# Prompt attention of a hybrid decoder layer: both heads of a pair in lock-step, in plain float32 on smaller tiles of the array

## The chip, the core and the metric

The kernel is one launch on one core of a Trainium2 chip. Its time is device time in microseconds (us), from the start to the end of an execution. TensorE (PE in the rows, its weight loads PEld) multiplies, VectorE (DVE), ScalarE (ACT) and GpSimd (POOL) work on elements, and SyncE (SP) issues DMAs. Matmul results land in PSUM, which this kernel cuts into eight banks of 128 partitions by 512 float32: two each of the tags `mm`, `S` and `T`, one each of `A` and `X`.

## The reference

One decoder layer over a prompt of 1024 tokens and 64 sample tokens (8 sequences of 8), width 1024: an input projection, 4 gated linear attention (GLA) heads, 8 softmax heads of width 64 with dilated windows, an output projection, a feed-forward network and norms, all in float32. The change concerns the softmax heads of the prompt:

```python
DILATED_PATTERNS = ((128, 1), (512, 4), (2048, 16))
def dilated_prompt(q, k, v):
    for (W, d) in DILATED_PATTERNS:
        ...
        s = jnp.einsum('brnqhe,brnkhe->brnhqk', qb, kk, preferred_element_type=F32)
        ...
        p = jnp.exp(s - m[..., None])
        den = jnp.sum(p, axis=-1)
        o = jnp.einsum('brnhqk,brnkhe->brnqhe', p.astype(vv.dtype), vv, preferred_element_type=F32)
        parts.append((back(m), back(den), o))
    return combine_patterns(parts)
```

The three patterns of a query are joined by their softmax denominators, so a single softmax over all keys gives the same, with a key that two patterns share counted twice; the kernel has these counts and the ALiBi slopes in a bias table.

## The kernel before, in words

The projection, the GLA heads, the output projection and the feed-forward network run as float32r matmuls of operands that are split in two parts, high and low (`mm3`, lines 203 to 205: high x high, low x high, high x low). The program is recorded through a scheduler that orders each engine's instructions ahead of time; each engine then runs its list in order and waits where an operand is late.

Softmax attention of the prompt goes over 4 pairs of heads (`attn_pair`), in a pair head by head (`for i in range(2)`), in a head over 4 groups `gq` of 256 queries, two tiles `qi` of 128 queries each. For a tile the *near* keys are the 256 keys of its own and the previous tile; the *far* keys are those up to 512 back that stand a multiple of 4 away, gathered by residue modulo 4 in `kres`, 32 per earlier tile and residue. A step of the loop does this:

- Scores into a bank `S`: near ones by two float32r matmuls on the whole array (L858, L859: the rows of the array hold the 64 high and 64 low parts of Q), far ones by four plain float32 matmuls, one for each residue, each into 32 columns of the array (L862).
- Softmax: DVE adds the bias and takes the maximum (L864), ACT the exponential and, with DVE's reciprocal, the scaling (L867 to L869).
- Transposes of the probabilities on TensorE into banks `T` (L881 near, L892 far); ACT copies them out as the high part and DVE subtracts for the low part (L883 and L884 near, L895 and L896 far).
- Values into bank `A`: float32r matmuls on the whole array with V's high and low halves side by side (L904 near, L910 far, once for the high and once for the low part of the probabilities). ACT and DVE add the two halves (L915, L918), and a DMA stores them to `o_dram`.

At a pair's start Q, K and V are split (ACT, DVE and POOL, L785 to L817), and the far values are read back from the output in memory (`vraw`, L839) and split (L841, L842).

Between these stand two other streams. `filler` yields the remaining units of the input projection and of the first half of the output projection, six `mm3` matmuls a unit; `fill_behind` lets so many units go behind a given matmul, at low priority. `sample_steps` does the softmax heads of the sample tokens (L951 key transposes, L959 scores, L995 values, with keys and values from cache by DMA into `raw`), two steps of it after each `gq` of a head.

Of the kernel before, what the change touches and what calls it, by code (L numbers as in the profile page):

```python
# [11 lines left out]
F32 = mybir.dt.float32  # L12
F32R = mybir.dt.float32r
# [24 lines left out]
FILL_START = (169, 202, 237, 277)  # L38
FILL_FROM = (164, 204, 240, 281)
FILL_TO = (199, 242, 273, 306)  # L40
# [4 lines left out]
FILL_STAGE = (1.0, 2.0, 3.0)  # L45
FILL_END = (26, 25, 19, 24)
# [59 lines left out]
def hymba_layer(  # L106
# [653 lines left out]
    PT = [[att.tile([P, 4, P], F32R, name=f"PT{part}{j}") for part in ("hi", "lo")] for j in range(2)]  # L760

    klo = [att.tile([P, T], F32R, name=f"klo{i}") for i in range(2)]
    Vf = att.tile([P, 2, 4, P], F32R, name="Vf")
    PF = {m: [att.tile([P, 2, P], F32R, name=f"PF{part}{m}") for part in ("hi", "lo")] for m in (P, 64)}
    for a in (klo[0][64:], klo[1][:64], Vf[64:, 1], PF[64][0][64:], PF[64][1][64:]):
        pool.memset(a.bitcast(F32), 0.0)

    def fill_upto(p, stage):
        part = (3 * (stage // 3) + FILL_STAGE[stage % 3]) / FILL_END[p]
        return FILL_FROM[p] + (FILL_TO[p] - FILL_FROM[p]) * min(1, part)  # L770

    def attn_pair(p):
        fs = slice(p * P, (p + 1) * P)
        fill(156 + 36 * p)
        fill_behind(latest[0], FILL_START[p])
        qr, kr, vr = (raws[p][name] for name in "qkv")
        Q, K, V = [], [], []
# [4 lines left out]
        for i in range(2):  # L782
            own, oth = slice(64 * i, 64 * i + 64), slice(64 - 64 * i, 128 - 64 * i)
            k = att.tile([P, T], F32R, tag="K", name="K", bufs=2)
# [3 lines left out]
            q = att.tile([P, T], F32R, tag="Q", name="Q", bufs=2)  # L788
            qv = q.rearrange("p (w r u) -> p w r u", r=4, u=32)
            src = qr[own, :T].rearrange("p (w u r) -> p w r u", r=4, u=32)  # L790
            for r in range(4):
                act(out=qv[own, :, r, :], in_=src[:, :, r, :], func=AF.Copy)
                vec.tensor_tensor(out=qv[oth, :, r, :], in0=src[:, :, r, :], in1=qv[own, :, r, :].bitcast(F32), op=ALU.subtract)
            K.append(k)
            Q.append(q)
            V.append(att.tile([P, NTT, P], F32R, tag="V", name="V", bufs=2))
# [3 lines left out]
        pool.tensor_copy(out=knew, in_=kr[:, T:])  # L800


        for t0 in range(0, NTT, 4):
            for src, dst in ((kr, ckp), (vr, cvp)):
# [3 lines left out]
                stg = smp.tile([P, 4, P], F32, tag="raw", name="stg", bufs=6)  # L808
                pv = ps.rearrange("p (t f) -> p t f", f=P)
                act(out=stg, in_=pv, func=AF.Copy)  # L810
                dma(out=dst[:, t0 : t0 + 4, fs], in_=stg)
                if src is vr:
                    for i in range(2):
                        hs = slice(64 * i, 64 * i + 64)
                        vhi = V[i][:, t0 : t0 + 4, 0:64]
                        act(out=vhi, in_=stg[:, :, hs], func=AF.Copy)
                        vec.tensor_tensor(out=V[i][:, t0 : t0 + 4, 64:128], in0=stg[:, :, hs], in1=vhi.bitcast(F32), op=ALU.subtract)  # L817
# [7 lines left out]
        dma(out=cvs[:, fs], in_=vnew)  # L825


        rows = cv_prompt[0, 0].rearrange("(c r) h e -> c r h e", r=4)

        fill_behind(last, FILL_FROM[p])  # L830

        sample = sample_steps(p, qbd, knew, vnew)
        for i in range(2):
            own, oth = slice(64 * i, 64 * i + 64), slice(64 - 64 * i, 128 - 64 * i)
            bias = att.tile([P, 480], F32, tag="bias", name="bias", bufs=1)
            dma(out=bias, in_=bias_p[2 * p + i])
            vraw = smp.tile([P, 2, 4, 64], F32, tag="raw", name="vraw", bufs=6)
            for cb, n in ((0, P), (1, 64)):
                dma(out=vraw[:n, cb], in_=rows[cb * P : cb * P + n, :, 2 * p + i])  # L839
                vh = Vf[:n, cb, :, 0:64]  # L840
                pool.tensor_copy(out=vh, in_=vraw[:n, cb])  # L841
                vec.tensor_tensor(out=Vf[:n, cb, :, 64:], in0=vraw[:n, cb], in1=vh.bitcast(F32), op=ALU.subtract)  # L842

            kres = att.tile([P, 4, 224], F32, tag="kres", name="kres", bufs=1)
            src = kr[own, : 4 * 224].rearrange("p (c r) -> p r c", r=4)
            pool.tensor_copy(out=kres[own], in_=src)
            pool.tensor_copy(out=kres[oth], in_=src)
            for gq in range(NTT // 2):
                Ps = []
                for qi in (2 * gq, 2 * gq + 1):  # L850
                    qs = slice(qi * P, (qi + 1) * P)
                    nf = 32 * qi if qi > 1 else 0
                    n = nf + (256 if qi else P)
                    k0 = max(qi - 1, 0) * P
                    sb = att.tile([P, 480], F32, tag="P", name="P", bufs=3)
                    st = att.tile([P, 3], F32, tag="st", name="st", bufs=4)
                    ps = bank("S")
                    mm(out=ps[:, nf : nf + 256], lhsT=Q[i][:, qs], rhs=K[i][:, k0 : k0 + 256], start=True, stop=False)  # L858
                    last_s = mm(out=ps[:, nf : nf + 256], lhsT=Q[i][:, qs], rhs=klo[i][:, k0 : k0 + 256], start=False, stop=True)  # L859
                    for r in range(4 if nf else 0):  # L860
                        q0 = qi * P + 32 * r
                        last_s = mm(out=ps[32 * r : 32 * r + 32, :nf], lhsT=Q[i][:, q0 : q0 + 32].bitcast(F32),  # L862
                                    rhs=kres[:, r, :nf], start=True, stop=True)
                    vec.tensor_tensor_reduce(  # L864
                        out=sb[:, :n], in0=ps[:, :n], in1=bias[:, 480 - n :] if qi else bias[:, 352:480], scale=-1.0,
# [359 lines left out]
```

## Time and profile before

| | |
|---|---|
| median of 3 runs | 1622.61 us (1622.34 to 1630.09) |
| profiled execution, its own time | 1624.35 us |
| its span, first to last instruction | 1622.6 us |
| PE busy | 1547.1 us, 95% of the span |
| PEld, DVE, ACT, POOL busy | 1429.8, 792.2, 491.2, 308.8 us |
| mean granted clock of TensorE | 0.972 of 2.4 GHz |

Busy time of PE counts each matmul until its results have left the array, so back-to-back matmuls overlap in it, and 95% doesn't mean that the array multiplies 95% of the time. What a matmul costs the next one is the distance between two starts. A plain float32 matmul stands in the trace as two records, a float32r matmul or a transpose as one.

### The profile page before, as it was taken

The page shows a single profiled execution, that of the slowest core. Times are in us where ns is not written, and L with a number is a line of the kernel's source. Part 1 is how long each engine was busy: PE and PEld are TensorE (multiplying, and loading weights), DVE is VectorE, ACT ScalarE, POOL GpSimd, SP SyncE. Part 2 cuts the span into 40 slices and gives each one's busy share as a digit, 9 for nine tenths or more (in the row PEclk, how much of TensorE's full clock was granted, in tenths as well). Part 3 has the DMA queues.
Part 4 walks back from the last instruction along what each step waited for, and adds up shares of the span by engine and source line. Part 5 has one row for each costly group of instructions (what it writes and reads, how often), then busy time and mean ns, then how long its engine had stood idle before and what let it go on. Part 6 is the DMA issues. An engine that isn't in the chain of part 4 may idle for free.

```text
span 1622.6 us, 28319 instructions
## 1 busy us (share of the span) xinstructions
PE 1547.1 (95%) x11696; PEld 1429.8 (88%) x11696; DVE 792.2 (49%) x1700; ACT 491.2 (30%) x995; POOL 308.8 (19%) x325
## 2 busy tenths in 40 slices
PE   7979999989899998998999999999999999999997
PEld 6768878888677876777999999999999999999997
DVE  5495575564534536345743444434344443434436
ACT  3143232145445456453522111121202112120213
POOL 1493342052213111100511000000100000010002
PEclk9998999989999998999999999999999999999998
DMA  5320121153353345666421021011102111110102
GB/s 151 97 70 28 30 67 42 42 147 108 91 135 103 87 127 169 181 172 200 122 79 53 26 66 49 30 53 40 53 27 65 41 38 53 37 55 27 53 1 111
DMA packets 180881, 126.71 MB, mean 78 GB/s; under 512 B 21104, under 2 KB 172560, under 8 KB 180752
## 3 DMA queue, kind: packets, MB, share of 16 engines
q1 hardware_dynamic: 176544, 124.69, 25.8%
q8 instruction: 92, 1.51, 0.4%
q10 hardware_dynamic: 4208, 0.21, 0.2%
q14 instruction: 37, 0.30, 0.1%
HBM read 101.40 MB, written 23.46 MB: 77 GB/s over the span
## 4 chain that ended last, share of the span: by engine, by line
PE 82%; DVE 8%; DMA 6%; issue 1%; POOL 1%; ACT 1%; SPq 0%; DVEq 0%; ACTq 0%; POOLq 0%
PE ps_mm L203 12%; PE ps_mm L204 12%; PE ps_mm L205 12%; PE ps_S L203 5%; PE ps_S L205 5%; PE ps_S L204 5%; PE ps_T L204 2%; PE ps_T L203 2%; PE ps_T L205 2%; DMA raw<-in_cache_swa_v_dram 2%; PE ps_A L910 2%; PE ps_A L205 1%; PE ps_A L203 1%; PE ps_A L204 1%; PE ps_X L204 1%
## 5 line engine op out<-in xcount | busy, mean ns | idle before, releaser
L203 PE MATMUL ps_mm<-xhi,whi 128*128 128x384 f32 (+1 forms) x576 | 202.3, 353 | 3.8 <-DVE raw_v L238 1.8
L1087 POOL TENSOR_TENSOR gt<-gt,ut 128x384 f32<-128x384 f32 (+1 forms) x66 | 64.0, 970 | 700.6 <-DVE ut L1086 700.6
L204 PE MATMUL ps_mm<-xlo,whi 128*128 128x384 f32 (+1 forms) x576 | 196.3, 342 | 0.2 <-DVE xlo L280 0.2
L205 PE MATMUL ps_mm<-xhi,wlo 128*128 128x384 f32 (+1 forms) x576 | 195.4, 341 | 0.6 <-DVE wlo L175 0.6
L203 PE MATMUL ps_mm<-hhi,whi 128*128 128x384 f32 (+1 forms) x528 | 173.5, 329 | 1.2 <-DVE gt L1084 1.2
L205 PE MATMUL ps_mm<-hhi,wlo 128*128 128x384 f32 (+1 forms) x528 | 173.7, 329 | 0.0
L204 PE MATMUL ps_mm<-hlo,whi 128*128 128x384 f32 (+1 forms) x528 | 173.6, 329 | 0.0
L203 PE MATMUL ps_S<-hhi,whi 128*128 128x384 f32 (+1 forms) x528 | 172.7, 327 | 0.0
L204 PE MATMUL ps_S<-hlo,whi 128*128 128x384 f32 (+1 forms) x528 | 172.7, 327 | 0.0
L205 PE MATMUL ps_S<-hhi,wlo 128*128 128x384 f32 (+1 forms) x528 | 172.5, 327 | 0.0
L203 PEld LDWEIGHTS ps_mm<-xhi,whi 128*128 128x128 f32 x576 | 112.2, 195 | 13.1 <-issue 5.6
L1085 ACT ACTIVATE gt<-gt 128x384 f32<-128x384 f32 (+1 forms) x66 | 33.1, 502 | 296.3 <-DVE gt L1084 296.3
L205 PEld LDWEIGHTS ps_mm<-xhi,wlo 128*128 128x128 f32 x576 | 112.0, 195 | 4.8 <-issue 2.6
L204 PEld LDWEIGHTS ps_mm<-xlo,whi 128*128 128x128 f32 x576 | 112.6, 196 | 3.8 <-issue 2.5
L1086 DVE TENSOR_TENSOR ut<-ps_S,rstd_bc 128x384 f32<-128x384 f32 (+1 forms) x66 | 35.4, 536 | 162.0 <-PE ps_S L205 162.0
L203 PEld LDWEIGHTS ps_mm<-hhi,whi 128*128 128x128 f32 x528 | 99.8, 189 | 1.4 <-DVE gt L1084 1.4
L205 PEld LDWEIGHTS ps_mm<-hhi,wlo 128*128 128x128 f32 x528 | 99.9, 189 | 0.0
L204 PEld LDWEIGHTS ps_mm<-hlo,whi 128*128 128x128 f32 x528 | 99.7, 189 | 0.0
L204 PEld LDWEIGHTS ps_S<-hlo,whi 128*128 128x128 f32 x528 | 99.2, 188 | 0.0
L203 PEld LDWEIGHTS ps_S<-hhi,whi 128*128 128x128 f32 x528 | 99.2, 188 | 0.0
L205 PEld LDWEIGHTS ps_S<-hhi,wlo 128*128 128x128 f32 x528 | 99.2, 188 | 0.0
L174 ACT ACTIVATE ghi<-gt 128x384 fp32r<-128x384 f32 (+1 forms) x66 | 33.5, 507 | 214.0 <-POOL gt L1087 214.0
(353 smaller groups left out, 3425.1 us busy)
## 6 DMA issues: line engine op xcount, KB each, us to landing
wraw<-in_w_in_dram SPq DMA_DIRECT2D x22, 512.0 KB, 3.8
wraw<-in_w_ffn_gate_dram SPq DMA_DIRECT2D x22, 512.0 KB, 3.6
wd_raw<-in_w_ffn_down_dram SPq DMA_DIRECT2D x22, 512.0 KB, 3.2
wuraw<-in_w_ffn_up_dram SPq DMA_DIRECT2D x22, 512.0 KB, 3.6
raw<-in_cache_swa_k_dram SPq DMA_DIRECT2D x32, 256.0 KB, 5.3
raw<-in_cache_swa_v_dram SPq DMA_DIRECT2D x32, 256.0 KB, 4.3
xa<-x_dram SPq DMA_DIRECT2D x32, 192.0 KB, 3.0
xr<-in_x_prompt_dram SPq DMA_DIRECT2D x8, 512.0 KB, 8.4
```

Of the source, the lines that this page charges most:

```text
L174: a = by.tensor_copy(out=hi, in_=raw) if by else act(out=hi, in_=raw, func=AF.Copy)
L203: mm(out=ps, lhsT=whi[k], rhs=xhi[k], start=first and k == 0, stop=False)
L204: mm(out=ps, lhsT=whi[k], rhs=xlo[k], start=False, stop=False)
L205: mm(out=ps, lhsT=wlo[k], rhs=xhi[k], start=False, stop=last and k == n - 1)
L910: mm(out=o, lhsT=Vf[:, cb, r, :], rhs=part[:, :, 32 * r : 32 * r + 32], start=False, stop=False)
L1085: act(out=gt, in_=gt, func=AF.Silu)
L1086: vec.tensor_tensor(out=ut, in0=pu[:, :n], in1=rstd_bc[:, cs], op=ALU.mult)
L1087: pool.tensor_tensor(out=gt, in0=gt, in1=ut, op=ALU.mult)
```

## The change

Both heads of a pair go through a step together. Q and K are no longer split: POOL reorders Q into `qres` (all 128 partitions, 64 a head) and K into `kres`, and the scores of the two heads are plain float32 matmuls on tiles of 64 rows by 32 columns, eight to a step: two heads (the array's rows) by four residues (its columns), into two banks `S`. The probabilities are copied out of the transposes once, and values are plain float32 matmuls on tiles of 128 rows by 64 columns, head 0 in the left half of the array and head 1 in the right half, both into one bank `A`. V is read where the transposes left it, and the far values are loaded for both heads at once. Softmax, transposes and the arithmetic on scores stay, as do the filler's 312 units; the marks at which they are let go are spread evenly, and the sample's steps come four to a `gq`.

```diff
+        qres = att.tile([P, T], F32, tag="qres", name="qres", bufs=2)
+        kres = att.tile([P, 4, 224], F32, tag="kres", name="kres", bufs=2)
+        for w in range(0, NTT, 4):
+            ws = slice(w * P, (w + 4) * P)
+            pool.tensor_copy(out=qres[:, ws].rearrange("p (w r u) -> p w r u", r=4, u=32),
+                             in_=qr[:, ws].rearrange("p (w u r) -> p w r u", r=4, u=32))
+        pool.tensor_copy(out=kres, in_=kr[:, : 4 * 224].rearrange("p (c r) -> p r c", r=4))
...
-            act(out=k[own], in_=kr[own, :T], func=AF.Copy)
-            pool.tensor_copy(out=k[oth], in_=kr[own, :T])
-            vec.tensor_tensor(out=klo[i][own], in0=kr[own, :T], in1=k[own].bitcast(F32), op=ALU.subtract)
...
-                act(out=qv[own, :, r, :], in_=src[:, :, r, :], func=AF.Copy)
-                vec.tensor_tensor(out=qv[oth, :, r, :], in0=src[:, :, r, :], in1=qv[own, :, r, :].bitcast(F32), op=ALU.subtract)
...
+        for cb, n in ((0, P), (1, 64)):
+            dma(out=vf[:n, cb], in_=rows[cb * P : cb * P + n, :, fs])
...
+        def scores(qi):
...
+            ps = [bank("S") for _ in heads]
+            for part in range(2 if nf else 1):
+                for r in range(4):
+                    rs = slice(32 * r, 32 * r + 32)
+                    for i, own in enumerate(heads):
+                        out = ps[i][rs, :nf] if part else ps[i][rs, nf:n]
+                        rhs = kres[own, r, :nf] if part else kr[own, k0 : k0 + near]
+                        ins = mm(out=out, lhsT=qres[own, qi * P + 32 * r : qi * P + 32 * r + 32], rhs=rhs, start=True, stop=True)
...
-                    mm(out=ps[:, nf : nf + 256], lhsT=Q[i][:, qs], rhs=K[i][:, k0 : k0 + 256], start=True, stop=False)
-                    last_s = mm(out=ps[:, nf : nf + 256], lhsT=Q[i][:, qs], rhs=klo[i][:, k0 : k0 + 256], start=False, stop=True)
...
+                if gq:
+                    act(out=av, in_=pv, func=AF.Copy)
...
+                    vec.tensor_copy(out=PF[m][i][:m], in_=ps[:m, 2 * cb * P : (2 * cb + 2) * P].rearrange("p (x q) -> p x q", x=2))
...
+                for i, own in enumerate(heads):
+                    last = mm(out=av[own, a:b], lhsT=V[:, kt, own], rhs=pt[i][:, e : e + (b - a) // P, :],
+                              start=j == 0, stop=j == len(steps) - 1)
+                for cb, m in far if j == 0 else ():
+                    for r in range(4):
+                        for i, own in enumerate(heads):
+                            o = av[own, :256].rearrange("p (x q) -> p x q", x=2)[:, :, 32 * r : 32 * r + 32]
+                            mm(out=o, lhsT=vf[:, cb, r, own], rhs=PF[m][i][:, :, 32 * r : 32 * r + 32], start=False, stop=False)
...
+                vec.tensor_copy(out=sum_[:, xs].rearrange("p (u r) -> p r u", r=4), in_=av[:, xs].rearrange("p (r u) -> p r u", r=4))
```

TensorE's list in the first pair, before, where scores and values of two steps meet (`PThi`, `PTlo`: near probabilities, `PFhi`, `PFlo`: far ones, `raw`: cached keys of the sample):

```order
L904 MATMUL ps_A<-PTlo_3833,V 128x256
L951 MATMUL ps_T<-ident,raw 128x128 x4
L910 MATMUL ps_A<-PFhi_3839,Vf 128x2x32
L858 MATMUL ps_S<-K,Q 128x256
L859 MATMUL ps_S<-klo_3834,Q 128x256
L862 MATMUL ps_S<-kres,Q 32x224 x3
L910 MATMUL ps_A<-PFlo_3840,Vf 128x2x32
```

and the same engine in the first pair now (L200 to L202 are the filler's lines, L835 scores, L890 far values, L933 the sample's key transposes):

```order
L202 MATMUL ps_mm<-xhi,wlo 128x320
L835 MATMUL ps_S<-raw_k,qres 32x256
L890 MATMUL ps_A<-PF_3834,Vf_3830 64x2x32
L933 MATMUL ps_T<-ident,raw 128x128 x4
L835 MATMUL ps_S<-raw_k,qres 32x256 x4
L890 MATMUL ps_A<-PF_3835,Vf_3830 64x2x32
```

Where only L862 stood on narrow tiles, every score and every value matmul does now, in two shapes, 64 by 32 and 128 by 64; one of a step's eight score matmuls stands alone ahead of a value matmul.

VectorE's list at the start of the first pair, before (`Q`, `klo`: low parts; `raw_v` is a filler unit's result on its way out of PSUM):

```order
L787 TENSOR_TENSOR klo_3834<-raw_k,K 64x1024
L175 TENSOR_TENSOR wlo<-wraw,whi 128x1024
L793 TENSOR_TENSOR Q<-raw_q,Q 64x8x32
L238 TENSOR_TENSOR raw_v<-ps_mm,rstd_bc 128x384
L793 TENSOR_TENSOR Q<-raw_q,Q 64x8x32 x3
L787 TENSOR_TENSOR klo_3835<-raw_k,K 64x1024
L793 TENSOR_TENSOR Q<-raw_q,Q 64x8x32 x4
```

and now, with buffer numbers (L840 is the softmax's first pass, L235 the filler's):

```order
L172 TENSOR_TENSOR wlo_3844<-wraw_3840,whi_3843 128x1024
L235 TENSOR_TENSOR raw_v_3847<-ps_mm_3848,rstd_bc_81 128x384
L840 ISA P_3956,st_3957<-ps_S_3946,bias_3942 128x128
L840 ISA st_3957 128x1
L840 ISA P_3962,st_3963<-ps_S_3947,bias_3944 128x128
```

The passes that split Q and K are gone from the list, and the first softmax passes follow the filler's result at once.

TensorE's list at the start of the last pair, now, with buffer numbers (`ps_S_7289` and `ps_S_7290` are the two heads of one step, `ps_S_7336` is head 0 of the next; L794 are the pair's own transposes):

```order
L794 MATMUL ps_T_7019<-ident_71,raw_v_5620 128x128 x4
L835 MATMUL ps_S_7094<-raw_k_5890,qres_7004 32x256 x4
L984 MATMUL ps_T_6938<-ident_71,avs_6936 128x128
L835 MATMUL ps_S_7289<-raw_k_5890,qres_7004 32x256 x4
L835 MATMUL ps_S_7289<-kres_7005,qres_7004 32x64 x4
L794 MATMUL ps_T_7026<-ident_71,raw_k_5890 128x128 x4
L835 MATMUL ps_S_7290<-raw_k_5890,qres_7004 32x256 x4
L835 MATMUL ps_S_7290<-kres_7005,qres_7004 32x64 x4
L794 MATMUL ps_T_7034<-ident_71,raw_v_5620 128x128 x4
L835 MATMUL ps_S_7336<-raw_k_5890,qres_7004 32x256 x4
```

Here the two heads don't stand together: each block of scores has one head, four tiles of the eight, and few other instructions lie between the blocks.

## Rows read from the trace of the kernel before

**Rows 1.** Busy time by stretch: attention, with the filler (start, length, engines, clock, DMA).
```profile
315.00:750.00 435.00, 407.84 (x3299) 333.73 (x3299) 205.89 (x536) 209.64 (x472) 91.23 (x89) 0.95 0.47 132
```
**Rows 2.** TensorE's waits in 315 to 750 us: total, times, longest, us.
```profile
PE ps_T L951 <- DMA raw<-in_cache_swa_k_dram: 4.0, 5, 1.2
PE ps_S L858 <- DVE Q L793: 3.3, 2, 2.7
...
PE ps_A L904 <- DVE PTlo L884: 2.7, 4, 1.2
...
PE ps_mm L203 <- DVE raw_v L238: 1.8, 1, 1.8
```
**Rows 3.** TensorE's groups by shape in 315 to 750 us.
```profile
L910 PE MATMUL ps_A<-PFhi,Vf 128*128 128x64 f32 x128 | 31.0, 270 | 0.0
...
L858 PE MATMUL ps_S<-K,Q 128*128 128x256 f32 x64 | 23.7, 372 | 6.4 <-DVE Q L793 3.3 <-DVE st L864 3.0
...
L904 PE MATMUL ps_A<-PThi,V 128*128 128x128 f32 x56 | 14.9, 287 | 0.0
...
L904 PE MATMUL ps_A<-PThi,V 128*128 128x256 f32 x32 | 11.9, 370 | 1.2 <-ACT PThi L883 1.2
...
L862 PE MATMUL ps_S<-kres,Q 128*32 128x224 f32 x64 | 8.3, 391 | 0.0
```
**Rows 4.** Timeline of TensorE, a run of far values (start us, duration us).
```profile
705.91 0.28 PE L910 MATMUL ps_A<-PFhi,Vf 128*128 128x64 f32 x1
...
706.58 0.42 PE L203 MATMUL ps_mm<-ohi,whi 128*128 128x384 f32 x1
```
**Rows 5.** The same timeline, a stream of plain float32 on four column tiles.
```profile
715.12 1.30 PE L995 MATMUL ps_X<-raw,pT 128*32 128x128 f32 x40
```
**Rows 6.** The same timeline, in and out of narrow tiles.
```profile
707.71 0.28 PE L858 MATMUL ps_S<-K,Q 128*128 128x256 f32 x1
707.83 0.28 PE L859 MATMUL ps_S<-klo,Q 128*128 128x256 f32 x1
708.04 0.37 PE L862 MATMUL ps_S<-kres,Q 128*32 128x96 f32 x8
708.34 0.39 PE L858 MATMUL ps_S<-K,Q 128*128 128x256 f32 x1
708.56 0.28 PE L859 MATMUL ps_S<-klo,Q 128*128 128x256 f32 x1
708.77 0.43 PE L862 MATMUL ps_S<-kres,Q 128*32 128x128 f32 x8
709.13 0.44 PE L982 MATMUL ps_T<-ident,sb 128*128 128x128 f32 x2
```
**Rows 7.** The same timeline in GLA: from one narrow shape to another.
```profile
225.45 0.76 PE L607 MATMUL ps_S<-Z 64*32 64x32 f32 x64
226.13 0.55 PE L677 MATMUL ps_T<-V,ktok 128*64 128x128 f32 x6
```
**Rows 8.** The same timeline in GLA: head 0's eight records on one tile, then head 1's.
```profile
97.59 0.96 PE L633 MATMUL ps_S<-Z 64*64 64x64 f32 x16 [0.41 <-DVE Z L625]
```
**Rows 9.** Timeline of VectorE at the start of attention.
```profile
349.42 3.60 DVE L793 TENSOR_TENSOR Q<-raw_q,Q 64x256 fp32r<-64x256 f32 x4
353.06 0.56 DVE L238 TENSOR_TENSOR raw_v<-ps_mm,rstd_bc 128x384 f32<-128x384 f32 x1
```
**Rows 10.** Timeline of TensorE there.
```profile
353.67 0.44 PE L203 MATMUL ps_mm<-xhi,whi 128*128 128x384 f32 x1 [1.83 <-DVE raw_v L238]
...
357.00 0.58 PE L858 MATMUL ps_S<-K,Q 128*128 128x256 f32 x1 [1.80 <-DVE st L864]
```
**Rows 11.** Busy time by stretch: two in which the granted clock fell.
```profile
356.20:366.40 10.20, 8.68 (x53) 6.60 (x53) 3.94 (x17) 5.23 (x15) 1.38 (x2) 0.50 0.71 180
...
438.10:448.40 10.30, 8.82 (x43) 7.42 (x43) 5.01 (x16) 5.53 (x16) 1.90 (x1) 0.50 0.27 78
```
**Rows 12.** VectorE's groups by shape, attention: a softmax pass.
```profile
L864 DVE CUSTOM_DVE_ANT_0 P<-ps_S,bias 128x256 f32<-128x256 f32 x8 | 3.4, 422 | 3.5 <-PE ps_T L892 3.5
```
**Rows 13.** GpSimd's groups by shape, attention: the reordering of K.
```profile
L846 POOL COPY kres<-raw_k 64x896 f32<-64x896 f32 x8 | 16.3, 2038 | 51.4 <-PE ps_S L862 51.4
```

More of the change, by code (lines that the diff above doesn't have):

```diff
@@ L807, in attn_pair @@
                     nc.tensor.transpose(out=ps[:, j * P : (j + 1) * P], in_=src[:, (t0 + j) * P : (t0 + j + 1) * P], identity=ident)
[L808 to L817, printed above, removed]
+                rows = V[:, t0 : t0 + 4] if src is vr else smp.tile([P, 4, P], F32, tag="raw", name="stg", bufs=6)
+                act(out=rows, in_=ps.rearrange("p (t f) -> p t f", f=P), func=AF.Copy)
+                dma(out=dst[:, t0 : t0 + 4, fs], in_=rows)
         ps = bank("T")
@@ L898, in attn_pair @@
-                fill_behind(last, fill_upto(p, 12 * i + 3 * gq + 1))
-                av = bank("A")
-                steps = [(2 * gq, 0, 256, 1)] + ([(2 * gq - 1, 0, P, 0)] if gq else []) + [(2 * gq + 1, P, 256, 3)]
-                for j, (kt, a, b, e) in enumerate(steps):
-                    for part in (hi, lo):
-                        last = mm(out=av[:, a:b], lhsT=V[i][:, kt, :], rhs=part[:, e : e + (b - a) // P, :],
-                           start=j == 0 and part is hi, stop=j == len(steps) - 1 and part is lo)
-                    for cb, m in far if j == 0 else ():
-                        for r in range(4):
-                            o = av[:, :256].rearrange("p (x q) -> p x q", x=2)[:, :, 32 * r : 32 * r + 32]
-                            for part in PF[m]:
-                                mm(out=o, lhsT=Vf[:, cb, r, :], rhs=part[:, :, 32 * r : 32 * r + 32], start=False, stop=False)
@@ L911, in attn_pair @@
-                fill_behind(last, fill_upto(p, 12 * i + 3 * gq + 2))
-                latest[0] = last
-                half = att.tile([P, 256], F32, tag="half", name="half", bufs=1)
-                sum_ = att.tile([P, 256], F32, tag="sum", name="sum", bufs=2)
-                act(out=half[own], in_=av[oth, :256], func=AF.Copy)
-                for x in range(2):
-                    vw = lambda a: a[own, x * P : x * P + P]
-                    vec.tensor_tensor(out=vw(sum_).rearrange("p (u r) -> p r u", r=4), in0=vw(av).rearrange("p (r u) -> p r u", r=4),
-                                      in1=vw(half).rearrange("p (r u) -> p r u", r=4), op=ALU.add)
@@ L920, in attn_pair @@
-                f0 = 512 + p * P + 64 * i
-                dma(out=o_dram[f0 : f0 + 64, gq * 256 : gq * 256 + 256], in_=sum_[own])
-                next(sample, None)
+                if gq:
+                    act(out=av, in_=pv, func=AF.Copy)
+                else:
+                    act(out=a[:, 1:4], in_=ps[:, P:].rearrange("p (e q) -> p e q", q=P), func=AF.Copy)
+                pt.append(a)
+            far = [(cb, min(P, 64 * gq - cb * P)) for cb in range(-(-64 * gq // P))]
+            for i in range(2 if far else 0):
+                ps = bank("T")
+                for cb, m in far:
+                    for x in range(2):
+                        last = nc.tensor.transpose(out=ps[:m, (2 * cb + x) * P : (2 * cb + x + 1) * P],
+                                                   in_=Ps[x][i][0][:, cb * P : cb * P + m], identity=ident)
+                    vec.tensor_copy(out=PF[m][i][:m], in_=ps[:m, 2 * cb * P : (2 * cb + 2) * P].rearrange("p (x q) -> p x q", x=2))
@@ new lines, in outputs @@
+            tick(last)
+            latest[0] = last
+            sum_ = att.tile([P, 256], F32, tag="sum", name="sum", bufs=2)
+            for x in range(2):
+                xs = slice(x * P, x * P + P)
+                vec.tensor_copy(out=sum_[:, xs].rearrange("p (u r) -> p r u", r=4), in_=av[:, xs].rearrange("p (r u) -> p r u", r=4))
+            dma(out=o_dram[512 + p * P : 512 + (p + 1) * P, gq * 256 : gq * 256 + 256], in_=sum_)
+        sample = sample_steps(p, qbd, knew, vnew)
+        for gq in range(NTT // 2):
+            Ps = [scores(2 * gq), scores(2 * gq + 1)]
+            outputs(gq, Ps)
+            for _ in range(4):
```

132 lines of the change are left out of this document (48 added, 84 removed).

## The prediction

> **What bounds the kernel now.** I read the stretches first. Attention and the filler that runs with it take 435 us, 315 to 750 us, at a mean clock of 0.95 [rows 1]; the change touches nothing outside. TensorE is busy for 408 of them, DVE for 206, ACT for 210, POOL for 91: TensorE's list bounds the stretch. Its waits come next [rows 2]: they are short and many, the cache's DMA 4.0 us for the keys, split operands that are late (`Q` 3.3, `PTlo` 2.7), and a filler result behind DVE's queue 1.8. So the question is what the same work costs on the array, by starts and not by busy time. The group list gives counts and shapes [rows 3], the timeline the prices [rows 4 to 8].
>
> **Prices.** A float32r matmul costs 0.112 us however few its columns: six far-value matmuls of 64 columns take 0.67 us from start to start [rows 4], and one of 256 columns takes 0.12 [rows 6]. Plain float32 on four column tiles goes through in ten steps of four records: 1.30 us less some 0.27 for the last to leave [rows 3, 5] is nine steps, 0.11 us a record of 128 columns. A matmul has two records, so a column costs 1.72 ns on its tile, and tiles of one shape run beside each other. A block of narrow matmuls therefore costs 1.72 ns times the columns of its busiest tile.
>
> Going in and out costs extra [rows 6]. L859 is followed after 0.21 us where 0.12 is usual (+0.09); the eight records of 96 columns should take 2 x 0.082 and the next starts after 0.30 (+0.14); that next one holds the array for 0.22 (+0.10). A round trip to float32r costs 0.33 us. Out to a transpose the middle part is 0.36 against 0.22, so 0.23 or more with the way in; I take 0.28. From one narrow shape to another [rows 7] the next start comes 0.08 us before the last block's end, where 0.16 is usual [rows 6]: 0.08, and I take 0.10. Its bounds are 0.08 and a whole trip, 0.33.
>
> **The change on the array.** I counted blocks along TensorE's lists, for the whole of attention.
>
> - Values. Before: 176 near and 256 far matmuls (the groups shown and their like) at 0.112, 48.4 us. Now: 64 blocks with 16,896 columns on the busiest tile, 29.1 us. That is -19.3. Far values carry it: their price was the 128-column weight load and not their 64 columns.
> - Scores. Before: 128 near matmuls at 0.112, 14.3 us, and 65 blocks of far ones with 9,824 columns, 16.9 us. Now 76 blocks with 19,232 columns, 33.1 us, so +1.9. If no block were broken up it would be 11,136 columns, 19.2 us; the list at the last pair's start shows why it isn't, one head at a time.
> - Trips. Before, 99 to float32r and 57 to transposes: 32.7 + 16.0 = 48.7 us. Now 80 and 96, 26.4 + 26.9, and 73 changes between narrow shapes at 0.10, 7.3: 60.6 us. +11.9, and from 5.8 - 48.7 + 53.3 = +10.4 to +28.7 by the bounds.
>
> Together -5.5 us. Filler, transposes and the sample's matmuls are the same in number and price.
>
> The Trainium skill has a rule that speaks against the change: TensorEngine Tiling (Array Packing), "Key Properties", says that changing the tiling mode drains TensorE, while tiles of one mode run independently. The trace agrees on entering and leaving (0.33 us); on a change between two narrow shapes it shows 0.08 and not a whole drain. By the rule taken at its word each of the 73 would cost 0.33, 16.8 us more; that is the fourth rival.
>
> **Waits.** At the start of attention DVE splits Q for 3.60 us in one run, and the filler's result `raw_v` stands behind it in DVE's queue [rows 9]; TensorE waits 1.83 us for that and 1.80 for the first softmax [rows 10]. DVE's list now has neither split. What takes their place is `qres` on POOL: K's 896 columns take 2.04 us there [rows 13], so 512 of Q take about 1.2, from a projection long done. I count the waits of `Q` and `raw_v`, 5.1 us [rows 2], as gone. Of `PTlo`'s 2.7 half stays, since ACT's copy is still ahead. -6.4.
>
> New are waits for the `S` banks. Both heads of a step now hold the two banks until DVE's first pass has read them, 0.42 us and 0.08 to read out for each head at 256 columns [rows 12], about 1.0 us for both. Behind the waiting matmul stands everything on TensorE, the sample's keys and the filler too. Between 24 of the 31 successive steps the list holds 2.3 us or more of other work, by the prices above; between seven it holds 0.7 or less, four of them in the last pair. Seven times 0.6 is +4; the bounds are 0 and 31 x 1.0.
>
> The far values are now read by TensorE from the loaded tile, with no split. The load stands on SP behind the store of V, and its first use is one `gq` later, so I cost it at nothing; SP's DMAs of the prompt's attention fall from 80 to 56. If that cover were gone, a wait as long as the cache's longest, 1.2 us [rows 2], in each pair: 5 us.
>
> **Clock.** A mean of 0.95 over 435 us means some 43 us at 1.2 GHz, half speed. Two falls of 10 us each come right after the waits at the start of attention and at the first change of pair [rows 11]. Work at half speed costs as much again, up to 22 us in all. The first follows waits that I count as gone; I take one fall, with what the new waits bring in set against it: -4, between -15 and +8.
>
> **Sum.** -5.5 - 6.4 + 4 - 4 = -11.9 us. The profiled execution took 1624.35 us, 1.75 more than its span and 1.74 above the median of the runs. From the median, 1622.6 - 11.9 is 1610.7. I predict 1611 us.
>
> **Rivals.**
>
> 1. The banks `S` decide: the steps run in lock-step with DVE. From 0.78 us at each of 31 gaps, 24 us in place of 4, the time passes 1630; at the full 1.0 us it is 1638. For it: seven gaps that are nearly empty, and blocks that alternate heads. Against it: the long gaps elsewhere, and a DVE that loses the split passes. 9%.
> 2. The array gives what I count, but waits and clock don't move, since the remaining waits (cache DMA) set the falls: -5.5 + 4 or so, 1617 to 1623. For it: the cache's waits are as long as `Q`'s [rows 2]. 22%.
> 3. The two heads don't run beside each other. Then the busiest column counts, 28,544 in place of 19,232, +16.0: 1627. The trace has head 0's and head 1's tiles side by side only at a hand-over [rows 8]: 16 records of 64 columns, 0.055 each, would take 0.88 + 0.22 in succession, and took 0.96. That they overlap at all speaks against it. 8%.
> 4. Changes between narrow shapes cost a whole trip: +16.8, 1628. Rows 7 speak against it. 5%.
> 5. More comes back: shorter chains behind ACT and DVE remove most falls of the clock, -10 to -15 in place of -4: 1600 to 1604, and below. For it: DVE had been the late engine at both falls. 15%.
>
> The forecast itself, 1605 to 1617, has 41%.
>
> **How the numbers follow.** A difference under about 0.5%, 8 us, can't be told from none here, so faster is under 1614.5 and slower over 1630.7. Faster: rival 5 and some 37 of the forecast's 41 points, 0.52. Slower: most of rival 1 and the upper ends of 3 and 4, 0.13. The rest, 0.35, is the same. The range leaves out a tenth at each side: from 1596, where two more falls of the clock are gone, to 1630, which takes in rivals 2 to 4.
>
> **What would show it.** In the profile after: far values at two records of some 0.055 us per 64 columns side by side; the eight score matmuls of a step starting within 0.1 us of each other, both heads, and the next start some 0.45 us after the block's first for 256 columns; attention's stretch 9 to 15 us shorter; no wait of TensorE for `raw_v` at its start and fewer low-clock stretches. It is wrong if the heads' records follow each other in time, if TensorE waits over 10 us in total for L840, or if the narrow blocks' changes cost more than 0.2 us each.

## The result

The changed kernel takes 1587.32 us (median of 4 runs, 1585.57 to 1589.02); the kernel before took 1624.47 beside it (4 runs). The ratio is 0.977, with a 95% interval from 0.975 to 0.980: 37 us faster, three times the forecast of 12, and below the range that was given. The direction was right and the size wrong.

The head of the page of the changed kernel:

```profile
span 1586.4 us, 28631 instructions
...
PE 1522.2 (96%) x12080; PEld 1377.2 (87%) x12080; DVE 717.3 (45%) x1556; ACT 435.6 (27%) x867; POOL 272.1 (17%) x296
```

TensorE is busy 25 us less (1547.1 before) although it has 384 records more. The stretches tell where the rest is. The next rows are those of the kernel before, from the first transpose of attention to its last matmul, and from there to the first matmul of the feed-forward part (start, length, busy time of PE, PEld, DVE, ACT, POOL, then clock, DMA share, GB/s):

```profile
315.10:743.60 428.50, 402.18 (x3259) 328.47 (x3258) 202.93 (x525) 208.15 (x469) 91.23 (x89) 0.95 0.47 132
743.60:812.70 69.10, 63.68 (x384) 61.54 (x384) 44.13 (x81) 34.64 (x69) 22.64 (x21) 1.00 0.51 156
```

and the same two of the changed kernel, which answer to [rows 1]:

```profile
308.50:710.00 401.50, 388.95 (x3691) 285.79 (x3691) 135.37 (x388) 154.11 (x344) 53.24 (x60) 0.98 0.51 142
710.00:778.10 68.10, 58.63 (x337) 57.46 (x336) 41.13 (x74) 33.55 (x65) 22.84 (x21) 0.95 0.49 151
```

Length minus busy time is TensorE's idle time: 31.7 us before, 22.0 now. At the low level the granted clock is 0.50, 1.2 GHz. The falls in these stretches are, before, the two of [rows 11] and

```profile
591.70:595.20 3.50, 3.50 (x21) 3.11 (x20) 0.79 (x3) 2.15 (x6) 0.00 (x0) 0.51 0.50 104
...
629.30:642.90 13.60, 11.58 (x54) 9.22 (x55) 10.07 (x28) 8.41 (x20) 1.36 (x4) 0.50 0.64 212
...
673.70:680.50 6.80, 5.22 (x24) 4.29 (x25) 3.62 (x11) 2.59 (x6) 0.15 (x1) 0.50 0.56 169
```

and now

```profile
631.70:635.10 3.40, 3.40 (x22) 2.74 (x10) 0.56 (x1) 0.53 (x1) 0.00 (x0) 0.50 0.47 126
679.50:689.70 10.20, 10.08 (x60) 5.96 (x60) 0.98 (x3) 0.00 (x0) 0.00 (x0) 0.50 0.28 82
727.20:734.00 6.80, 4.07 (x13) 4.07 (x14) 1.70 (x4) 1.55 (x4) 0.00 (x0) 0.50 0.02 6
```

As the cost of low clock I count half of TensorE's busy time in them (at the low level the 384-column matmuls of a filler unit start 0.32 us apart, otherwise 0.17): 37.8 us busy before and 17.6 now, so 18.9 and 8.8. Idle time in a fall is counted as idle time only. What is left is work: 447.0 and 438.8. Together 497.6 and 469.6, 28.0 us less. I use this split for every kernel below. Another 6.6 us lie ahead of attention, where the two programs are the same, and 1.6 behind it.

TensorE's waits before, 315 to 812.6 us (total, times, longest), where [rows 2] leaves them out:

```profile
PE ps_X L995 <- DMA raw<-in_cache_swa_v_dram: 4.1, 5, 1.4
...
PE ps_mm L203 <- ACT ohi L174: 3.6, 2, 2.3
...
PE ps_S L858 <- DVE st L864: 3.0, 3, 1.8
PE ps_mm L203 <- DVE xa L520: 2.9, 1, 2.9
...
PE ps_T L892 <- DVE osT L1007: 1.8, 2, 1.3
```

and in the changed kernel, 308 to 779 us, which answer to [rows 2]:

```profile
PE ps_mm L200 <- ACT ohi L171: 9.1, 4, 6.7
PE ps_X L977 <- DMA raw<-in_cache_swa_v_dram: 2.9, 2, 1.9
PE ps_T L933 <- DMA raw<-in_cache_swa_k_dram: 2.6, 1, 2.6
PE ps_A L890 <- DVE PF L876: 2.0, 1, 2.0
PE ps_T L863 <- ACT stg L796: 2.0, 1, 2.0
```

No wait of the score matmuls (L835) for their banks is in the whole list; nor is one for `raw_v`, for the softmax pass (`st` L864, 3.0 us before) or for the projection's `xa` (2.9 before). The projection's operand `ohi` is waited for longer, 9.1 us against 3.6: that is given back.

The groups that take the place of [rows 3], and the timeline that shows their price (start, duration):

```profile
L835 PE MATMUL ps_S<-raw_k,qres 64*32 64x256 f32 x448 | 31.4, 388 | 0.0
...
L884 PE MATMUL ps_A<-PT,V 128*64 128x256 f32 x64 | 20.7, 405 | 0.0
...
L890 PE MATMUL ps_A<-PF,Vf 128*64 128x64 f32 x256 | 16.7, 237 | 2.0 <-DVE PF L876 2.0
```
```profile
445.94 0.66 PE L933 MATMUL ps_T<-ident,raw 128*128 128x128 f32 x4
446.53 0.66 PE L835 MATMUL ps_S<-raw_k,qres 64*32 64x256 f32 x16
446.98 0.43 PE L835 MATMUL ps_S<-kres,qres 64*32 64x160 f32 x2
447.35 0.32 PE L941 MATMUL ps_X<-kT,qbd 128*32 128x128 f32 x4
```

Sixteen records of 256 columns are eight matmuls, four of each head. From their start to the next is 0.45 us, as forecast; one matmul alone should take 256 x 1.72 = 0.44, and two on each of four tiles 0.88. So the eight tiles run beside each other, both heads too. One matmul of 160 columns should take 0.28 and the next shape starts after 0.37: a change between narrow shapes costs 0.09. Over the whole attention the medians are 0.09 there, 0.09 into narrow tiles, 0.20 out to float32r and 0.15 out to a transpose.

### The profile page after: what moved, and what is told of

It is laid out like the page before. It is cut to its first block, busy times and chain, and to the rows that moved or that the text cites. A ratio compares the mean times of both kernels' runs of the same rounds, so it can differ in the third digit from the quotient of the medians.

```text
span 1586.4 us, 28631 instructions
## 1 busy us (share of the span) xinstructions
PE 1522.2 (96%) x12080; PEld 1377.2 (87%) x12080; DVE 717.3 (45%) x1556; ACT 435.6 (27%) x867; POOL 272.1 (17%) x296
## 4 chain that ended last, share of the span: by engine, by line
PE 86%; DMA 5%; DVE 5%; POOL 1%; issue 1%; ACT 1%; SPq 0%; DVEq 0%; ACTq 0%; POOLq 0%
PE ps_mm L200 13%; PE ps_mm L201 12%; PE ps_mm L202 12%; PE ps_S L202 5%; PE ps_S L201 5%; PE ps_S L200 5%; PE ps_T L201 2%; PE ps_T L200 2%; PE ps_T L202 2%; PE ps_S L835 2%; DMA oraw<-o_dram 2%; PE ps_T L933 2%; PE ps_X L977 2%; PE ps_A L202 1%; PE ps_A L200 1%; PE ps_A L201 1%
## 5 line engine op out<-in xcount | busy, mean ns | idle before, releaser
L200 PE MATMUL ps_mm<-xhi,whi 128*128 128x384 f32 (+1 forms) x576 | 199.5, 347 | 2.0 <-ACT whi L171 1.6
L202 PE MATMUL ps_mm<-xhi,wlo 128*128 128x384 f32 (+1 forms) x576 | 194.6, 339 | 1.1 <-DVE wlo L172 1.1
L200 PE MATMUL ps_mm<-hhi,whi 128*128 128x384 f32 (+1 forms) x528 | 172.8, 327 | 1.2 <-DVE gt L1066 1.2
L202 PE MATMUL ps_mm<-hhi,wlo 128*128 128x384 f32 (+1 forms) x528 | 173.0, 328 | 0.0
L200 PE MATMUL ps_S<-hhi,whi 128*128 128x384 f32 (+1 forms) x528 | 172.7, 327 | 0.0
L202 PE MATMUL ps_S<-hhi,wlo 128*128 128x384 f32 (+1 forms) x528 | 172.5, 327 | 0.0
L200 PEld LDWEIGHTS ps_mm<-xhi,whi 128*128 128x128 f32 x576 | 110.2, 192 | 13.6 <-issue 7.6
L202 PEld LDWEIGHTS ps_mm<-xhi,wlo 128*128 128x128 f32 x576 | 110.2, 191 | 7.3 <-issue 4.8
L200 PEld LDWEIGHTS ps_mm<-hhi,whi 128*128 128x128 f32 x528 | 99.2, 188 | 1.4 <-DVE gt L1066 1.4
L202 PEld LDWEIGHTS ps_mm<-hhi,wlo 128*128 128x128 f32 x528 | 99.2, 188 | 0.0
L202 PEld LDWEIGHTS ps_S<-hhi,wlo 128*128 128x128 f32 x528 | 99.2, 188 | 0.0
L200 PEld LDWEIGHTS ps_S<-hhi,whi 128*128 128x128 f32 x528 | 99.2, 188 | 0.0
L1090 DVE TENSOR_TENSOR h<-h,ps_T 128x384 f32<-128x384 f32 (+1 forms) x120 | 63.5, 529 | 68.1 <-PE ps_T L202 68.1
```

The costliest lines, as they stand in the source:

```text
L200: mm(out=ps, lhsT=whi[k], rhs=xhi[k], start=first and k == 0, stop=False)
L202: mm(out=ps, lhsT=wlo[k], rhs=xhi[k], start=False, stop=last and k == n - 1)
L1090: vec.tensor_tensor(out=h[:, k, cs], in0=h[:, k, cs], in1=ps[:, :n], op=ALU.add)
```

## The experiments

The prices just given make a count possible for any kernel here: TensorE's instruction list, each block at its busiest tile, each change of shape at its price. "Counted" below means this. The table comes first, since the readings use it. All but the first column are from the profiled execution, over the two stretches shown above, in us.

| kernel | median | start | length | idle | low clock | work |
|---|---|---|---|---|---|---|
| before | 1624 | 315.1 | 497.6 | 31.7 | 18.9 | 447.0 |
| changed | 1587.3 | 308.5 | 469.6 | 22.0 | 8.8 | 438.8 |
| after2 | 1591.8 | 313.6 | 468.0 | 18.2 | 11.6 | 438.3 |
| b_nosplit | 1615.5 | 310.8 | 493.0 | 24.6 | 21.5 | 447.0 |
| b_nolo | 1600.8 | 310.7 | 474.1 | 25.9 | 13.6 | 434.7 |
| b_sum_q2 | 1608.0 | 313.3 | 484.4 | 22.2 | 18.1 | 444.1 |
| b_nolo_q | 1601.8 | 315.0 | 476.4 | 25.5 | 20.2 | 430.6 |
| a_heads | 1613.5 | 313.7 | 484.6 | 17.3 | 7.6 | 459.7 |
| a_pair | 1594.9 | 309.5 | 473.7 | 23.5 | 10.8 | 439.4 |
| a_passes | 1622.4 | 315.0 | 498.8 | 37.2 | 22.5 | 439.1 |
| a_passes_q2 | 1620.8 | 315.1 | 496.0 | 36.6 | 19.5 | 439.9 |
| a_passes_q3 | 1612.7 | 315.3 | 490.3 | 28.1 | 20.6 | 441.6 |
| after_q | 1585.9 | 310.3 | 461.4 | 22.3 | 9.9 | 429.2 |
| a_block2 | 1578.5 | 309.6 | 453.2 | 20.5 | 10.7 | 422.0 |
| a_block3 | 1557.7 | 314.1 | 433.6 | 20.7 | 4.5 | 408.3 |
| a_block3_q2 | 1562.2 | 308.3 | 441.2 | 22.9 | 9.9 | 408.4 |

The two profiles of the changed kernel (changed, after2) differ by 3.8 us in idle time and 2.8 in low clock, so less than that is not read. A profiled execution can lie off its kernel's median: b_nolo's is 5.9 us below it, a_block2's 5.3, a_heads's 4.9, after_q's 3.8, and a_passes_q3's 3.4 above. Beside the runs below the kernel before took 1623.4 to 1626.9 us (medians).

**Is the gain ahead of attention the change's?** after2 is the changed kernel, unedited.

> The changed kernel once more, unchanged. Theory A (the 6.6 us by which attention starts earlier, 308.5 against 315.1 us, are a clock fall that comes or stays away from execution to execution, and not the change): the start of attention moves by some us between the two executions of one kernel, up to 6.8 us, one fall more or less ahead of it. Rival (something in the changed program moves it): the start is again within 1 us of 308.5 us, with the same falls at 103, 116, 144 and 249 us. Total 1585 to 1590 us.

Measured: 1591.76 us in one run, just over the 1590 given, with attention's start at 313.6. Here falls of the clock stand at 211.5 and 252.4 us for 6.8 us each, where the first profile had one of 3.4 at 249.4. So the 6.6 us belong to the execution and not to the change; the stretch that the change touches is 28.0 and 29.6 us shorter in the two profiles.

**Take the passes away.** In the kernel before, b_nolo leaves out every VectorE pass that makes a low part for the prompt's attention (the filler's stay); b_nosplit only those at the pair starts. The low tiles are set to zero once:

```diff
-            vec.tensor_tensor(out=klo[i][own], in0=kr[own, :T], in1=k[own].bitcast(F32), op=ALU.subtract)
-                vec.tensor_tensor(out=qv[oth, :, r, :], in0=src[:, :, r, :], ...)
-                        vec.tensor_tensor(out=V[i][:, t0 : t0 + 4, 64:128], ...)
-                vec.tensor_tensor(out=Vf[:n, cb, :, 64:], ...)
 # b_nolo also:
-                    vec.tensor_tensor(out=lv[:, xs, ys_, :], in0=pv[:, xs, ys_, :], ...)
-                        vec.tensor_tensor(out=flo[:m], in0=pv, ...)
```

> The kernel before, with its float32r operands and its matmuls, all of them, but without VectorE's passes that make low parts: those tiles are set to zero once, so the low parts are left out of the sums. Theory A (the 9.7 us of waits and 10.1 us of low clock that the change saved beyond the array work hang on these passes): idle time of TensorE in the attention stretch falls from 31.7 to 20 to 24 us, the low-clock time from 44 us towards 20 us, and the total to 1605 to 1612 us. Rival B (they hang on the lock-step, half as many steps with twice the cover): no more than 4 us come off, 1620 to 1626 us.

Measured: 1600.81 us, ratio 0.987 (0.985 to 0.990), 22.6 us less than before. More than theory A gave, and it came in another way: in the profile idle falls by 5.8, to 25.9 where 20 to 24 was given, low clock by 5.3, and the work by 12.3 although every matmul is still there. The list shows why. With fewer passes to wait for, the program's scheduler breaks the blocks up less (TensorE goes into narrow tiles 138 times instead of 155, for far scores and the sample's matmuls), and the count gives 12.0 less. Of the waits that don't name a removed pass not all went:

```profile
PE ps_X L991 <- DMA raw<-in_cache_swa_v_dram: 5.0, 7, 1.2
...
PE ps_mm L203 <- DVE xa L520: 3.8, 3, 1.8
PE ps_T L947 <- DMA raw<-in_cache_swa_k_dram: 3.6, 4, 2.2
...
PE ps_S L856 <- DVE st L862: 1.4, 4, 0.6
```

`st` and `osT` (0.6) are shorter than before, but cached keys and values are waited for 8.6 us (8.1 before) and `xa` 3.8 (2.9).

> The kernel before without VectorE's low-part passes at the pair starts alone (queries, keys, values, distant values: those low parts are zero and left out of the sums); the low parts of the probabilities, made in each step, stay. Without both kinds the kernel before took 1600.8 us. Counted from the instruction order, work and switches are 0.5 us under the kernel before (without both kinds 12.0 us under it, since the steps' blocks are then less broken up). Theory A1 (a good half of the 22.6 us hangs on the step passes, which break up the order and hold PT, the pair starts only make a few waits): 1613 to 1619 us. Theory A2 (the long passes at pair starts, 12.4 us of VectorE per pair, are what everything queues behind): 1608 us or less.

Measured: 1615.46 us, ratio 0.994 (0.992 to 0.997): 11.5 us, as A1 has it. The work is where the count puts it, within 0.5 us. The passes in the steps are worth the other 11.

**Put them back.** a_pair and a_passes write keys, queries and values a second time on ACT and VectorE; a_passes also the probabilities (and it has the queries ahead of the keys; the lines below show a_pair's order):

```diff
+        for i, own in enumerate(heads):
+            act(out=kr[own, :T], in_=kr[own, :T], func=AF.Copy)
+            vec.tensor_copy(out=kr[own, :T], in_=kr[own, :T])
+            for r in range(4):
+                act(out=qv[own, :, r, :], in_=src[own, :, r, :], func=AF.Copy)
+                vec.tensor_copy(out=qv[own, :, r, :], in_=src[own, :, r, :])
 ...
+                    vec.tensor_copy(out=av, in_=pv)          # a_passes only
```

> The changed kernel with passes of the kernel before put back as second writings of the same values: per pair 8 ACT and 8 VectorE passes over the queries, 2 and 2 over the keys, 4 and 4 over the values, and in each step a VectorE pass behind each ScalarE copy of the transposed probabilities (and an ACT one ahead of VectorE's for the distant ones), on which the matmuls wait. TensorE's work is unchanged. Theory A: waits and clock falls come back, 1597 to 1608 us, with PE idle in the attention stretch at 30 us or above. Rival B (lock-step covers them): 1585 to 1591 us.

> The changed kernel with only the pair-start passes put back (second writings of keys, queries and values on ACT and VectorE), none in the steps; with both kinds it took 1622.4 us. Work and switches by the order: 0.6 us under the changed kernel. Theory A1: 1594 to 1602 us, the smaller part of the 35 us. Theory A2: 1610 us or more, with PE idle in attention and projection at 32 us or above.

Measured: a_passes 1622.37 us, a_pair 1594.92. With the passes back, the whole gain is gone (ratio to before 0.998, 0.996 to 1.000), beyond the 1608 of theory A, though work is within 1 us of the changed kernel's: idle is up by 15 to 19 us and low clock by 11 to 14. a_pair's 7.6 us are the smaller part, and in its profile one wait of 6.9 us is for the second writing of the keys. So lock-step covers none of it, rival B falls, and most of it sits in the steps. In a_passes TensorE's list of waits has the prompt's probabilities nowhere; it begins with this:

```profile
PE ps_X L994 <- DMA raw<-in_cache_swa_v_dram: 14.1, 7, 7.8
PE ps_S L847 <- DVE raw_k L785: 6.5, 1, 6.5
```

If a late pass is paid for in a transfer, the queue that issues the transfers should show it; that is tested next.

**Where the transfers stand.** All these DMAs are in SP's list, in order. In the kernel before, SP's own waits (same columns, 315 to 814 us) say what it stands for ahead of L921, the store of the finished sums:

```profile
SPq L921 <- DVE sum L918: 32.6, 11, 8.2
SPq L921 <- DVE Vf L842: 19.5, 2, 10.4
```

and at a change of pair its timeline shows what stands behind (L811 stores the prompt's keys and values, L940 loads cached keys), with TensorE beside it:

```profile
551.93 0.38 SPq L811 DMA_DIRECT2D out_dram<-stg  x1
555.02 0.48 SPq L921 DMA_DIRECT2D o_dram<-sum  x1
555.59 1.12 SPq L811 DMA_DIRECT2D out_dram<-stg  x2
...
561.11 3.08 SPq L940 DMA_DIRECT2D raw<-in_cache_swa_k_dram  x5
```
```profile
565.68 0.66 PE L951 MATMUL ps_T<-ident,raw 128*128 128x128 f32 x4 [0.57 <-DMA raw<-in_cache_swa_k_dram]
567.34 0.63 PE L951 MATMUL ps_T<-ident,raw 128*128 128x128 f32 x4 [1.01 <-DMA raw<-in_cache_swa_k_dram]
...
569.48 0.63 PE L951 MATMUL ps_T<-ident,raw 128*128 128x128 f32 x4 [1.16 <-DMA raw<-in_cache_swa_k_dram]
```

Nothing is issued from 552.3 to 555.0, the keys are asked for at 561.1, and TensorE waits for them three times. b_sum_q2, after_q, a_passes_q2 and a_block3_q2 move that one store:

```diff
-            dma(out=o_dram[...], in_=sum_)
+            nc.gpsimd.dma_start(out=o_dram[...], in_=sum_)
```

> The kernel before with only that store moved to POOL's queue. SP's queue stood 32.6 us ahead of it for the sums and 27.3 us more there for other VectorE passes; TensorE waited 8.2 us for cached keys and values. By the order 2.8 us less work and switches. Theory Q: cached keys and values are waited for under 4 us, 1611 to 1619 us. Rival R: 1620 to 1628 us.

Measured: 1607.99 us, ratio 0.990 (0.985 to 0.994), 16 us less with every pass still in place, and below the 1611 of theory Q. The same change of pair now has the keys' load half a microsecond behind L811's store:

```profile
548.96 0.38 SPq L811 DMA_DIRECT2D out_dram<-stg  x1
549.44 3.09 SPq L940 DMA_DIRECT2D raw<-in_cache_swa_k_dram  x3
```

TensorE waits 1.8 us for cached keys and values where it was 8.1:

```profile
PE ps_X L995 <- DMA raw<-in_cache_swa_v_dram: 1.4, 3, 0.8
...
PE ps_T L951 <- DMA raw<-in_cache_swa_k_dram: 0.4, 1, 0.4
```

Idle falls by 9.5 and work by 2.9, as counted (2.8). So in the kernel before nearly a third of the idle time came through this store. What SP stood for `Vf` stays: 22.1 us, now ahead of L940. In the kernel before the cached keys and values share their six `raw` buffers with the copies of K and V and with the far values, in the changed kernel with the copies of K alone; no run tries that by itself.

> The changed kernel with all passes put back (1622.4 us), and the store of the finished sums issued from POOL's queue instead of SP's. In the version before, TensorE's longest waits were for cached values (14.1 us, longest 7.8) and SP's queue stood 40.3 us ahead of that store, waiting for VectorE. Theory Q (the passes delay the sums, the store blocks SP, the cached values behind it come late, and idle and low clock follow): those waits fall under 6 us and the total to 1600 to 1612 us. Rival R (the passes cost by themselves, the queue is a bystander): 1617 to 1626 us.

Measured: 1620.80 us. Theory Q fails here: cached values are still waited for, 12.7 us. SP now stood 37.0 us ahead of another store (of the sample's result) and 20.7 for the landing of the projection's stores.

> The changed kernel with all passes put back and now three things on POOL's queue: the store of the sums, and the projection stream's loads and stores of its running sums, ahead of which SP's queue still stood (21.7 us for the landing of earlier stores, the 7.8 us wait for cached values right behind one of them). Theory Q (it is SP's queue, whichever transfer stands in it): cached values are waited for under 5 us and 1598 to 1612 us. Rival R (the passes' work itself): 1617 us or more.

The loads and stores of `xa` go to POOL's queue too (two more `dma_start` of that kind). Measured: 1612.65 us, 10 less than a_passes: just above theory Q's 1612 and short of rival R. Cached values are waited for 8.2 us instead of 14.1, in short pieces (longest 1.7). The queue carries part of the 35 us; 25 of them stay unexplained by it.

> The kernel before with both cures at once: no low-part passes (low parts zero, left out of the sums; alone 1600.8 us, 22.6 off) and the store of the sums on POOL's queue (alone 1608.0 us, 16 off). If they take different waits (the passes hold queries and probabilities, the store holds cached keys and values): near the sum, 1584 to 1592 us, as fast as the changed kernel without any of its tiles. If they are two names of one wait: 1598 to 1604 us.

Measured: 1601.82 us, ratio 0.987 (0.983 to 0.992): the cures don't add up. In this profile the work fell once more (430.6), but against b_nolo idle and low clock did not, and TensorE waited 7.6 us for cached keys and values (8.6 in b_nolo) with SP standing 29.7 us ahead of the sample's store. Either cure takes 16 to 23 us, both take 22.

> The changed kernel with only that store moved to POOL's queue. If the change already took away what the store held up in the kernel before (PE waited 8.2 us for cached keys and values there, 5.5 and 4.2 in two profiles of the changed one): 1583 to 1590 us, no more than the 5.1 us that the order counts less. If the store holds it up as much as before: 1570 to 1578 us.

Measured: 1585.86 us (1582.08 to 1590.15), 1.5 under the changed kernel, within the spread of both: what the store held up, the change had already taken. Cached keys and values are waited for 6.1 us, no less than in the changed kernel, so this store holds them up no more.

**What lock-step does.** a_heads has the changed kernel's arithmetic and passes, one head behind the other:

```diff
-            ps = [bank("S") for _ in heads]
+            ps = bank("S")
-                for i, own in enumerate(heads):
+                for i, own in ((h, heads[h]),):
 ...
+        for h in range(2):
+            for gq in range(NTT // 2):
+                Ps = [scores(h, 2 * gq), scores(h, 2 * gq + 1)]
+                outputs(h, gq, Ps)
```

> The changed kernel's arithmetic without lock-step: one head of the pair after the other, so score blocks use half of the row tiles and value blocks half of the columns at a time. Counted from the order with the changed kernel's prices: score blocks 42.6 instead of 31.8 us, value blocks 38.8 instead of 27.6 us, all work and switches 24.3 us more. Theory A (lock-step saves array time, the cover of its longer steps is of little account): 1608 to 1616 us. Rival B (lock-step also halves the number of steps that wait for softmax, so waits and clock come back too): 1622 us or more.

Measured: 1613.53 us, 26 more than the changed kernel, and work is up by 20.9 where the count said 24.3. Idle (17.3) and low clock (7.6) are as low as in lock-step. So waits and clock don't hang on lock-step, which is worth array time alone; without it, plain float32 costs 13 us of work more than the split operands did.

**Keep the blocks whole.** In the changed kernel scores and values still come in pieces. a_block2 puts the head whose bank comes later first and pins the other matmuls of a call behind it; a_block3 does so for the sample's eight matmuls too:

```diff
-                    for i, own in enumerate(heads):
+                    for i, own in ((1, heads[1]), (0, heads[0])):
 ...
                         ins = mm(out=out, lhsT=qres[...], rhs=rhs, start=True, stop=True)
+                        if (part, r, i) != (0, 0, 1):
+                            tc.keep_in_program_order(ins)
```

> The changed kernel with the matmuls of one score call, of one value call and of one sample step kept behind one another in TensorE's order, the head whose bank or operand comes later first. Counted from the instruction order with the changed kernel's measured prices (0.093 us into narrow tiles, 0.150 to transposes, 0.198 to float32r, 0.092 between narrow shapes): stays in narrow tiles fall from 243 to 161, blocks of work by 12.9 us, switches by 15.4 us, so 28 us less, 1559 us, if nothing new waits. Rival (each block now waits for its later operand with nothing else to issue, as the scheduler had filled those gaps with the split halves): 1575 us or more, with PE idle up by what is missing.

Measured: 1557.65 us (1556.56 to 1558.73), ratio to before 0.960 (0.958 to 0.961). The count said 1559. Work is down by 30.5 for 28 counted, and idle is no higher. A sample step's eight matmuls (L945, sixteen records) now go through in one block:

```profile
443.67 0.64 PE L945 MATMUL ps_X<-kT,qbd 128*32 128x128 f32 x16
444.24 1.09 PE L937 MATMUL ps_T<-ident,raw 128*128 128x128 f32 x8
```

Both score banks must be free at once here, and yet TensorE waits for them once, 1.5 us.

> The changed kernel with score and value matmuls kept together, but the sample steps left as they are. By the order 15.3 us less than the changed kernel (work 9.6, switches 5.8), where the version with the sample steps kept together too counted 28 us and took 1557.7 us, 30 us less. If the count tells: 1571 to 1575 us. Rival (most of the 30 us were the sample steps' blocks and a lucky clock): 1580 us or more.

Measured: 1578.54 us (1573.28 to 1581.43): between the two readings. Work is 16.8 down for 15.3 counted, but the median only 8.8; the profiled run is the lowest of the four, at 1573.3, and what the other three lost is not shown.

> The changed kernel with blocks kept together (1557.7 us) and the store on POOL's queue. By the order 1.9 us more work and switches. TensorE's waits for cached keys and values were 2.0 us there, so little is left to take: 1555 to 1561 us by both theories; under 1553 us would mean that SP's queue held back more than the waits show.

Measured: 1562.20 us, 4.5 above a_block3, just over the 1561 given. Work is the same; low clock is 5 us more. Nothing was left to take in the queue. a_block3 is the fastest kernel here, 30 us under the changed one.

## Why the prediction was wrong

By its own steps, on the two profiles of the changed kernel (28.0 and 29.6 us less in the stretch; the forecast was 11.9):

- **Array, -5.5.** Right in direction, 3 us short: -8.2 and -8.7. The price by the busiest tile, the 0.10 for a change between narrow shapes (0.09) and the broken-up score blocks stand. The trips were priced too high, 0.33 and 0.28 us where the medians above give 0.29 and 0.24; with these, and 0.09 between narrow shapes, they come to +10.4 in place of +11.9. The rest was not taken apart. Rivals 3 and 4 fall, the first by the eight tiles of one block, the second by the 0.09: a change between narrow shapes has a price, but not that of a whole trip. The Trainium skill (TensorEngine Tiling (Array Packing), "Key Properties") says that a change of the tiling mode drains TensorE; the trace agrees in that every change into, out of or between narrow shapes has a price, 0.09 us or more.
- **`Q`, `raw_v` and `PTlo`, -6.4.** Right in the main: the first two waits went, 5.1 us. `PTlo`'s 2.7 us came back under another name, `PF`, 2.0 us and 3.3 in the second profile.
- **New waits for the S banks, +4.** This failed: there is none. I priced the hand-over with the other work of the list at its full rate, and saw seven gaps too short for it; none of the seven waits. Rival 1 falls with it.
- **What I left at nothing.** This failed too. Net idle was to fall by 2.4 and fell by 9.7 and 13.5; of the 7.3 and 11.1 us that the sum lacks, the largest gap of the three, 4 are the bank waits and the rest is here. I credited a wait only where its row names a removed pass. But the waits for `st` (3.0), `xa` (2.9) and `osT` (1.8) went too, and those for cached keys and values fell from 8.1 to 5.5 and 4.2. With the passes back (a_passes) idle time rises by 15 to 19 us, of which only 6.5 have a row that names such a pass. For the cache b_sum_q2 shows a way: SP's queue stood for VectorE's sums, and 6.3 us went with that store. It was in the trace: SP's waits for VectorE, which I had not read. The other side doesn't show it: without the passes b_nolo has 5.8 us less idle time, no more than the rows that name them (`Q` 3.3, `PTlo` 2.7), and still waits for `xa` and the cache. So why `xa` went is open.
- **Clock, -4.** Mis-sized: -10.1 and -7.3. I allowed one fall. After the start of attention the changed kernel has no low clock until 631.7 us, where the kernel before had four falls by then, the two of [rows 11] among them. This is the way of rival 5, to which I gave 15%: its -10 was reached in one profile of the two, and the result lies below the 1600 to 1604 worked out for it since idle time and work fell more as well. Rival 2 falls with it.
- **Ahead of attention, nothing.** 6.6 us of the two profiles' difference lie there, behind the same instructions; after2 gives 5.1 of them back with the clock falls that differ. That part is no gain of the change.

The whole is also shown by parts: no passes, one head at a time, 1613.5; lock-step on top, 1587.3; the same with the passes back, 1622.4.

Open: why the passes put back cost 35 us when leaving them out of the kernel before gave 22.6, and when three transfers taken out of SP's queue returned only 10. The passes put back are not those of the kernel before: they write over what is already there, behind POOL's reordering, so the chains are longer. The evenly spread marks of the filler were not tried alone either; with them and the passes (a_passes) idle time is 37.2 us, so by themselves they don't bring the gain. And low clock goes along with idle time in the table, but not evenly: b_nosplit has 21.5 us of it beside 24.6 idle, a_pair 10.8 beside 23.5, and b_nolo and b_nolo_q have the same idle time with 13.6 and 20.2. What a fall hangs on is not shown.

## What to carry to other kernels

When passes on a helper engine go, don't credit only the waits that name them: read the waits of the queue that issues the transfers, and follow each one to what stands behind it. Here that gave 16 us in the kernel before, though only 10 of the 35 in the kernel with the passes put back. On the array, count the blocks of narrow tiles in the instruction list and price each by its busiest tile and its changes of shape; that count was within 4.5 us of the work in every kernel here where it was made beforehand, and it pointed to the 30 us that keeping the blocks whole brought.

## What was not expected of the hardware

Eight plain float32 matmuls on 64x32 tiles run at the time of one (0.45 us for 256 columns, where the price per column gives 0.44 for one alone), and a change between narrow shapes costs no more than entering one (0.09 us both). The falls of the clock differ between executions of one program, here by several microseconds: attention began at 308.5 and at 313.6 us behind the same instructions.
